# Attention's values, queries and keys kept split in DRAM, its mask tables made by GpSimd in the first FFN, and the softmax division on VectorE

## The chip, the core and the metric

The kernel runs on one core of one Trainium2 chip. The core has a matrix engine (TensorE, PE in the profile), a vector engine (VectorE, DVE), an activation engine (ScalarE, ACT), a general engine (GpSimd, POOL), a queue engine (SyncE, SP) that here only issues transfers, and 16 DMA engines. Each engine takes its instructions strictly in order, and waits on semaphores for the others. The metric is the device time of one execution in microseconds, as the median of several runs.

## What is computed

One layer of an encoder on 1024 tokens of width 1024, all in float32. The part that the change touches is the token mixer:

```python
h = h + 0.5 * swiglu(rms_norm(h, ffn1_norm), ffn1_w_gate, ffn1_w_up, ffn1_w_down)
u = rms_norm(h, mix_norm)
q, k, v, s_in, gates = split(u @ w_in)            # 512, 512, 512, 512, 2048 columns
y_attn = neighbourhood_attention(q, k, v, na_rpb) @ w_attn_out
y_ssm = s5_branch(s_in, ...) @ w_ssm_out
g_attn, g_ssm = split(sigmoid(gates))
h = h + (g_attn * y_attn + g_ssm * y_ssm) @ w_out
h = h + 0.5 * swiglu(rms_norm(h, ffn2_norm), ffn2_w_gate, ffn2_w_up, ffn2_w_down)
h = h + (p @ ple_w_proj) * sigmoid(rms_norm(h, ple_norm) @ ple_w_gate)
return rms_norm(h, final_norm)
```

The tokens are a grid of 16 rows by 64 columns. In neighbourhood_attention each of 8 heads of 64 dimensions lets a token see a window of 8 rows by 16 columns, clamped at the grid's edge, with a learned bias by relative position:

```python
bias = rpb[:, dr_idx[:, None, None], dc_idx[None]]
sc = einsum('bchd,brcwhd->bhcrw', qr, kn) * scale + bias
pr = softmax(sc)                                   # over the 8 x 16 window
out = einsum('bhcrw,brcwhd->bchd', pr, vn)
```

## The kernel before

A float32 product is made of three matmuls on operands that are split in two: hi, a rounded copy (CAST on ScalarE), and lo, the rest (a subtraction on VectorE), and then hi by hi, lo by hi and hi by lo (`mm3`, lines 184 to 186; `split`, lines 153 and 154). So each weight or activation tile costs one ScalarE and one VectorE operation before TensorE can use it. The first FFN runs from 0 to about 645 us, the mixer's projections, attention and SSM to about 1100 us, the merge and the output projection behind them, then the second FFN and the rest.

*The FFN* (`Ffn.run`) works through a list of items. In its second half an item is "B", one of 7 products by one of 11 blocks of the down projection: 12 matmuls on one tile araw (read back from a_d, split into ah and al) and one tile of weights (wblk, combined by additions in lines 422 and 424, then split into wh and wl). Each loop turn first issues the loads of items up to 7 ahead, then the preparation of items up to 4 ahead, then the item's matmuls, with a call of `tick()` after each three.

*Side work.* `tick()` counts down for one Python generator, which yields the number of ticks until its next piece. In the first FFN that generator is `gen_all`, which makes the SSM's tables with GpSimd (lines 918 to 933), pair by pair. In the mixer it is the attention and SSM generator: for each pair of heads and each unit of 16 it records a score (two matmuls, s), a softmax, a transposition (pt) and, two to five units later, the product with the values (O). The order in PE, DVE and ACT follows what the recording and the scheduler made of it.

*The mixer.* The values are made token tile by token tile (8 tiles of 24 matmuls, lines 1392 to 1394), copied by ScalarE into vs and stored in v_d. The query and key projections of a head pair follow (`qk_proj`), between tiles of the gates (gt). Queries and keys stay in SBUF: qs holds a head's high half in one half of the partitions and its low half in the other, and kh and kl hold the key's halves twice. For each head and column block `load_v` reads vf from v_d and splits it into vhl. `make_tabs` makes for each of the 16 units of 8 heads and 2 row blocks the bias and mask tables: row = bt + rowm (128 x 384), and three times tb = row + colm (288, 384 and 288 elements used), on VectorE in lines 1186 and 1193. A unit is then: s, the sum with tb and the maximum (L1211), the exponential (L1214), the reciprocal (L1215), the division as a ScalarE copy with a scale (L1216). During the first part of attention GpSimd runs the SSM's recurrence, 128 steps of three operations (`scan_steps`, lines 1092 to 1094), and in the last quarter `ssm_out` copies its states to xs and makes yo.

Rings matter here: `st` has 3 buffers of 128 x 1024 (staged weights, wst), `w` has 12 of 128 x 1024 (qs, kh, kl, weights, xs), and `tmp` has 4.

Of the kernel before, what the change touches and what calls it, by code (L numbers as in the profile page):

```python
# [16 lines left out]
P = 128  # L17
SEQ = 1024
# [11 lines left out]
KC0 = (0, 8, 24, 40)  # L30
KNC = (24, 32, 32, 24)
KVAR = (0, 1, 1, 2)
KF0 = (8, 0, 0, 0)
NEG = -1.0e30
PRI = 300

# [2 lines left out]
def encoder_block(ctx, tc, I, out):  # L39
# [35 lines left out]
    def tw(name, shape=(P, 1024), dt=F32R):  # L75
        return at("w", shape, dt, name)
# [13 lines left out]
    def dtile(name, shape):  # L90
        return dr.tile(list(shape), F32, name=name)
# [96 lines left out]
    def hsl(t):  # L188
        return slice(t * HT, (t + 1) * HT)
# [554 lines left out]
        return vecs.pop()  # L744

    def gconst(name, shape):
        return pools["g"].tile(list(shape), F32, name="g_" + name)

    def exp_parts(x, nm):

# [19 lines left out]
    def gen_params():  # L770
# [209 lines left out]
    def gen_all():  # L980
        while "g" not in pools:
            yield 1
        yield from gen_params()
        load_bc(0)
        yield 10
        for pr in range(NPAIR):
            fin = gen_pair(pr)
            yield 25 if pr < NPAIR - 2 else 40
            fin()
            yield 4  # L990

    def store_h(m, t):
        nc.scalar.dma_start(h_d[:, (2 * m + t) * HT:(2 * m + t + 1) * HT], h[m][t])
# [1 line left out]
    u, done, u_first, u_second = halves(h, 1, store_h)  # L995

    def t0_done():
        start(u_first())

    ffn = Ffn(s7, I["wg1"], I["wu1"], I["wd1"], a1_d, load_x, done, t0_done, (4, 7))  # L1000
# [122 lines left out]
        return go  # L1123


    rowm = const("rowm", [P, 2, 12])
    colm = const("colm", [P, 3, 32])
    nc.sync.dma_start(rowm, I["rowm"])
    nc.sync.dma_start(colm, I["colm"])
    vdr = v_d.rearrange("(r c) d -> r c d", c=GRID)  # L1130
    qkv = {}
    vld, tabs = {}, {}

    def qk_proj(hp, wq, wk):
        qs, kh, kl = [], [], []
        for t in range(2):
            o = proj(wq, t, "q")
            for i in range(2):
                if t == 0:
                    qs.append(tw("qs"))  # L1140
                src = o[i * 64:(i + 1) * 64].rearrange("p (r b c) -> p r b c", r=8, b=4)
                hs, ls = slice(i * 64, (i + 1) * 64), slice((1 - i) * 64, (2 - i) * 64)

                def view(sl):
                    return qs[i][sl, hsl(t)].rearrange("p (b r c) -> p r b c", b=4, r=8)
                A.copy(view(hs), src)
                V.tensor_tensor(view(ls), src, view(hs).bitcast(F32), ALU.subtract)
        for t in range(2):
            o = proj(wk, t, "k")
            for i in range(2):  # L1150
                if t == 0:
                    kh.append(tw("kh"))
                    kl.append(tw("kl"))
                hs, ls = slice(i * 64, (i + 1) * 64), slice((1 - i) * 64, (2 - i) * 64)
                A.activation(kh[i][hs, hsl(t)], o[hs], AF.Copy, scale=0.125)
                A.activation(kh[i][ls, hsl(t)], o[hs], AF.Copy, scale=0.125)
                for s_ in (hs, ls):
                    V.scalar_tensor_tensor(kl[i][s_, hsl(t)], o[hs], 0.125, kh[i][hs, hsl(t)].bitcast(F32),
                                           ALU.mult, ALU.subtract)
        for i in range(2):  # L1160
            qkv[2 * hp + i] = (qs[i], kh[i], kl[i])

    def load_v(hd, cb):
        n = 4 * KNC[cb]
        vf = tmp("vf", [P, 4, 64])
        for g in range(4):
            nc.sync.dma_start(vf[0:n, g],
                              vdr[4 * g:4 * g + 4, KC0[cb]:KC0[cb] + KNC[cb], hd * 64:(hd + 1) * 64])
        hl = thid("vhl", [P, 4, 2, 64])
        A.copy(hl[0:n, :, 0], vf[0:n])  # L1170
        V.tensor_tensor(hl[0:n, :, 1], vf[0:n], hl[0:n, :, 0].bitcast(F32), ALU.subtract)
        vld[hd, cb] = hl

    bts = {}

    def load_bias(b):

        if b < 2 * NH:
            e0 = 4 - 4 * (b % 2)
            bts[b] = ap_.tile([P, 12, 32], F32, tag="bt", bufs=1, name="bt")  # L1180
            nc.sync.dma_start(bts[b].rearrange("p r c -> p (r c)"), I["rpbw"][b // 2, :, e0 * 32:(e0 + 12) * 32])

    def make_tabs(hd, rb):
        b = 2 * hd + rb
        row = tmp("row", [P, 12, 32])
        V.tensor_tensor(row, bts.pop(b),
                        rowm[:, rb].unsqueeze(2).broadcast_to([P, 12, 32]), ALU.add)
        load_bias(b + 1)
        res = []
        for v in range(3):  # L1190
            n, f0 = (24, 32, 24)[v], (8, 0, 0)[v]
            tb = ap_.tile([P, 12, 32], F32, tag="tb", bufs=3, name="tb")
            V.tensor_tensor(tb[:, :, 0:n], row[:, :, f0:f0 + n],
                            colm[:, v, f0:f0 + n].unsqueeze(1).broadcast_to([P, 12, n]), ALU.add)
            res.append(tb)
        tabs[hd, rb] = res

    def attn_scores(hd, rb, cb):
        q, kh, kl = qkv[hd]
        n = KNC[cb]  # L1200
        nk = 12 * n
        qv = q[:, rb * HT + cb * P:rb * HT + (cb + 1) * P]

        def kv(kt):
            return kt.rearrange("p (r c) -> p r c", c=GRID)[:, 4 * rb:4 * rb + 12, KC0[cb]:KC0[cb] + n]
        s3 = bank("s")[:, 0:nk].rearrange("p (r c) -> p r c", c=n)
        T.matmul(s3, lhsT=qv, rhs=kv(kh), start=True, stop=False)
        T.matmul(s3, lhsT=qv, rhs=kv(kl), start=False, stop=True)
        sm = thid("sm", [P, 384], F32)[:, 0:nk]
        st = ap_.tile([P, 4], F32, tag="stat", bufs=4, name="stat")  # L1210
        V.tensor_tensor_reduce(out=sm.rearrange("p (r c) -> p r c", c=n), in0=s3,  # L1211
                               in1=tabs[hd, rb][KVAR[cb]][:, :, 0:n], scale=-1.0, scalar=3.0e38,
                               op0=ALU.add, op1=ALU.min, accum_out=st[:, 0:1])
        A.activation(sm, sm, AF.Exp, bias=st[:, 0:1], scale=-1.0, accum_out=st[:, 1:2])  # L1214
        V.reciprocal(st[:, 2:3], st[:, 1:2])  # L1215
        A.activation(sm, sm, AF.Copy, scale=st[:, 2:3])  # L1216
        return sm

    def attn_turn(cb, sm):
# [10 lines left out]
    def attn_values(hd, rb, cb, O, ph, pl):  # L1230
        kp = 4 * KNC[cb]
        hl = vld[hd, cb]
        for g in range(3):

            T.matmul(O[:, ksl(cb)], lhsT=hl[0:kp, rb + g].rearrange("p h d -> p (h d)"), rhs=ph[0:kp, ksl(g)], start=(g == 0), stop=False,
                     skip_group_check=True)
            T.matmul(O[0:64, ksl(cb)], lhsT=hl[0:kp, rb + g, 0], rhs=pl[0:kp, ksl(g)], start=False, stop=(g == 2),
                     skip_group_check=True)
        if cb == 3:
            ot, ol = tmp("ot"), tmp("ol")  # L1240
            A.copy(ol[0:64], O[64:128])
            V.tensor_tensor(ot[0:64].rearrange("p (r b c) -> p b r c", r=8, b=4),
                            O[0:64].rearrange("p (b r c) -> p b r c", b=4, r=8),
                            ol[0:64].rearrange("p (b r c) -> p b r c", b=4, r=8), ALU.add)
            nc.scalar.dma_start(o_d[hd * 64:(hd + 1) * 64, hsl(rb)], ot[0:64])
# [40 lines left out]
    def mixer_side():  # L1286
# [6 lines left out]
        for pr in range(NPAIR):  # L1293
# [7 lines left out]
                ld[pr + 1] = inject_load(pr + 1)  # L1301
            inject(pr, *ld.pop(pr))
            yield 3
        while 0 not in qkv:
# [12 lines left out]
        SO = 48  # L1317
        for j in range(n + 6):
            if j < n:
                hd, rb, cb = units[j]  # L1320
                while hd not in qkv:
                    yield 1
                if cb == 0 and j > 0:
                    make_tabs(hd, rb)
# [61 lines left out]
    for tt in range(NK):  # L1386
        o = bank("v")
        t, c0 = tt // 4, (tt % 4) * P
        for k in range(NK):
# [3 lines left out]
            T.matmul(o, lhsT=xh, rhs=wl, start=False, stop=False)  # L1393
            T.matmul(o, lhsT=xl, rhs=wh, start=False, stop=(k == NK - 1))
            tick()
        vs = tmp("vs")
        A.copy(vs, o)
        nc.scalar.dma_start(v_d[tt * P:(tt + 1) * P, :], vs)

    def load_br(t, b):  # L1400

# [30 lines left out]
            res += [(hi[:, ksl(k)], lo[:, ksl(k)]) for k in range(4)]  # L1432
        return res

    gm = 2
    for hp in range(4):
        wq, wk = loadw(win[hp]), loadw(win[4 + hp])
        w = loadw(win[16 + gm])
        qk_proj(hp, wq, wk)
        n = 2 if hp < 3 else 6  # L1440
        for i in range(n):
            wn = loadw(win[17 + gm]) if i < n - 1 else None
            for t in range(2):
                gate_tile(w, gm, t)
            gm += 1
            w = wn
    W = [loadw(win[16 + m]) for m in (14, 15)]
    for i in range(2):
        gate_tile(W[i], 14 + i, 0)
# [360 lines left out]
```

## Time and profile before

| | |
|---|---|
| median of 3 runs | 2099.88 us (2098.8 to 2100.49) |
| profiled execution, span | 2094.5 us |
| runs' median above that span | 5.4 us |
| TensorE busy | 2074.5 us |
| VectorE, ScalarE, GpSimd busy | 1416.1, 999.6, 399.4 us |
| DMA | 285.19 MB, mean 136 GB/s |

The span is what the profiler saw from the first to the last instruction of one execution; a run's time has a few microseconds around it. In the views a row names the line of the kernel, the engine, the operation, the tile written and the tiles read, the shape, and how often; "idle before" is the engine's gap just ahead, with what ended it. A matmul is listed with 0.39 us though the next one starts 0.23 us later, since they are pipelined.

### The profile page before, as it was taken

The numbers are of one execution on the slowest core, as the hardware profiler recorded it, in microseconds if no ns is written. First come the engines' busy times: TensorE is split into PE (matmuls) and PEld (weight loads), VectorE is DVE, ScalarE is ACT, GpSimd is POOL, SyncE is SP. The second block draws the span as 40 slices with busy tenths as digits, with TensorE's granted clock in tenths as the row PEclk, the third lists the DMA queues.
The fourth block names the chain that finished last, engine by engine and source line by source line (L and its number), as shares of the span: only waits on it lengthen the run. The fifth ranks groups of instructions, "written<-read, shape, count | busy, mean of one in ns | idle before, by whom it ended". The sixth has DMA issues, their size and how long they took to land.

```text
span 2094.5 us, 28063 instructions
## 1 busy us (share of the span) xinstructions
PE 2074.5 (99%) x9662; PEld 1705.4 (81%) x9662; DVE 1416.1 (68%) x2420; ACT 999.6 (48%) x1832; POOL 399.4 (19%) x636
## 2 busy tenths in 40 slices
PE   8999999999999999999999999999999999999998
PEld 3788888888888888888898888788888888888886
DVE  7897776667967334677753668995665665786855
ACT  6434333334445333667774635643333334445543
POOL 0037556441000006888200001000000000000000
PEclk9999999999999999999999999999999999999999
DMA  3435444475533551233477745243324238433302
GB/s 134 143 118 154 125 135 120 144 270 169 188 114 111 159 189 64 70 97 98 123 208 260 247 145 117 77 150 121 100 86 135 82 121 297 155 106 94 118 21 81
DMA packets 197744, 285.19 MB, mean 136 GB/s; under 512 B 41569, under 2 KB 81121, under 8 KB 197601
## 3 DMA queue, kind: packets, MB, share of 16 engines
q1 hardware_dynamic: 180304, 258.20, 38.8%
q10 hardware_dynamic: 14992, 21.00, 3.0%
q0 software_dynamic: 2304, 4.20, 1.2%
q8 instruction: 76, 1.25, 0.2%
q14 instruction: 68, 0.55, 0.1%
HBM read 201.01 MB, written 82.31 MB: 135 GB/s over the span
## 4 chain that ended last, share of the span: by engine, by line
PE 94%; DVE 2%; ACT 1%; DMA 1%; SPq 0%; issue 0%; DVEq 0%; ACTq 0%
PE dx L184 4%; PE dx L185 4%; PE dx L186 4%; PE gx L184 3%; PE ux L184 3%; PE ux L186 3%; PE gx L186 3%; PE gx L185 3%; PE ux L185 3%; PE gt L184 3%; PE gt L185 3%; PE gt L186 3%; PE dy L186 2%; PE dy L184 2%; PE dy L185 2%; PE gy L184 2%
## 5 line engine op out<-in xcount | busy, mean ns | idle before, releaser
L153 ACT CAST wh<-hbuf 128x512 fp32r<-128x512 f32 x280 | 173.0, 622 | 392.3 <-PE gx L185 80.9
L154 DVE TENSOR_TENSOR wl<-hbuf,wh 128x512 fp32r<-128x512 f32 x280 | 209.2, 750 | 122.7 <-ACT wh L153 120.5
L153 ACT CAST wh<-wblk 128x512 fp32r<-128x512 f32 x190 | 118.0, 622 | 192.6 <-PE dx L185 83.2
L154 DVE TENSOR_TENSOR wl<-wblk,wh 128x512 fp32r<-128x512 f32 x190 | 130.6, 690 | 49.3 <-ACT wh L153 41.8
L184 PE MATMUL dx<-ah,wh 128*128 128x512 f32 x416 | 163.3, 393 | 0.3 <-DVE hbuf L688 0.3
L186 PE MATMUL dx<-ah,wl 128*128 128x512 f32 x416 | 161.9, 389 | 0.0
L185 PE MATMUL dx<-al,wh 128*128 128x512 f32 x416 | 161.8, 389 | 0.0
L1092 POOL TENSOR_TENSOR sc<-X,rho 128x128 f32<-128x128 f32 x128 | 77.9, 609 | 327.2 <-ACT X L1075 317.3
L154 DVE TENSOR_TENSOR al<-araw,ah 128x512 fp32r<-128x512 f32 x154 | 106.3, 694 | 50.1 <-PE dx L185 21.1
L184 PE MATMUL gx<-xh,wh 128*128 128x512 f32 x320 | 124.9, 390 | 1.2 <-DVE c L575 1.2
L184 PE MATMUL ux<-xh,wh 128*128 128x512 f32 x320 | 125.0, 390 | 0.0
L186 PE MATMUL ux<-xh,wl 128*128 128x512 f32 x320 | 124.5, 389 | 0.0
L185 PE MATMUL gx<-xl,wh 128*128 128x512 f32 x320 | 124.5, 389 | 0.0
L186 PE MATMUL gx<-xh,wl 128*128 128x512 f32 x320 | 124.5, 389 | 0.0
L185 PE MATMUL ux<-xl,wh 128*128 128x512 f32 x320 | 124.5, 389 | 0.0
L153 ACT CAST ah<-araw 128x512 fp32r<-128x512 f32 x154 | 94.9, 619 | 43.2 <-PE dx L185 12.6
L184 PE MATMUL gt<-xh,wh 128*128 128x512 f32 x256 | 102.7, 401 | 0.0
L186 PE MATMUL gt<-xh,wl 128*128 128x512 f32 x256 | 99.8, 390 | 0.0
L185 PE MATMUL gt<-xl,wh 128*128 128x512 f32 x256 | 99.8, 390 | 0.0
L422 DVE TENSOR_TENSOR hbuf<-hbuf 128x512 f32<-128x512 f32 x120 | 91.4, 762 | 2.1
L184 PEld LDWEIGHTS dx<-ah,wh 128*128 128x128 f32 x416 | 78.1, 188 | 17.8 <-issue 0.7
L185 PEld LDWEIGHTS dx<-al,wh 128*128 128x128 f32 x416 | 78.1, 188 | 16.9 <-issue 0.7
(381 smaller groups left out, 5590.2 us busy)
## 6 DMA issues: line engine op xcount, KB each, us to landing
araw<-a_d SPq DMA_DIRECT2D x154, 256.0 KB
a_d<-c SPq DMA_DIRECT2D x148, 256.0 KB
wblk<-in_wd SPq DMA_DIRECT2D x88, 256.0 KB
hbuf<-in_wg SPq DMA_DIRECT2D x40, 512.0 KB
hbuf<-in_wu SPq DMA_DIRECT2D x40, 512.0 KB
wst<-in_win SPq DMA_DIRECT2D x26, 512.0 KB
hbuf<-in_xT SPq DMA_DIRECT2D x32, 256.0 KB
h_d<-hbuf ACTq DMA_DIRECT2D x32, 256.0 KB
```

Of the source, the lines that this page charges most:

```text
L153: A.copy(hi, src)
L154: return eng.tensor_tensor(lo, src, hi.bitcast(F32), ALU.subtract)
L184: T.matmul(o, lhsT=wh, rhs=xh, start=first, stop=False, skip_group_check=more)
L185: T.matmul(o, lhsT=wh, rhs=xl, start=False, stop=False, skip_group_check=more)
L186: T.matmul(o, lhsT=wl, rhs=xh, start=False, stop=last, skip_group_check=more)
L422: V.tensor_tensor(b11, (b12, b22, None, None, b21)[i - 2], b11, ALU.subtract)
L1092: G.tensor_tensor(sc, both, rho4, ALU.mult)
```

## The change

Four things change. Values, queries and keys are split once, straight behind their projections, and stored as halves: v_d doubles in width, q_d and k_d are new, and attention loads the halves (vhl, qs, kh, kl) from there without any copy. The value tile vs is now 128 x 1024 and comes from the `st` ring. The mask tables are made by GpSimd in the first FFN, behind the SSM's tables, stored in t_d, and loaded by attention (`load_tabs`). The division of the softmax moves from ScalarE to VectorE. And the order of query and key projections and gate tiles becomes a list, `todo`, in which the second head pair is projected earlier.

```diff
@@ -112,7 +115,10 @@
-    v_d = dtile("v_d", [SEQ, 512])
+    v_d = dtile("v_d", [SEQ, 1024])
+    q_d = dtile("q_d", [4, 2, P, SEQ])
+    k_d = dtile("k_d", [4, 2, P, SEQ])
+    t_d = dtile("t_d", [2 * NH, P, TABS])
@@ -877,6 +883,25 @@
+    def load_bias(b):
+
+        e0 = 4 - 4 * (b % 2)
+        bt = pools["g"].tile([P, 12, 32], F32, tag="tg", bufs=1, name="bt")
+        nc.sync.dma_start(bt.rearrange("p r c -> p (r c)"), I["rpbw"][b // 2, :, e0 * 32:(e0 + 12) * 32])
+        return bt
+
+    def gen_tabs(b, bt):
+
+        rb = b % 2
+        row = pools["g"].tile([P, 12, 32], F32, tag="em", bufs=1, name="row")
+        G.tensor_tensor(row, bt, gen["rowm"][:, rb].unsqueeze(2).broadcast_to([P, 12, 32]), ALU.add)
+        for v in range(3):
+            n, f0 = TN[v], TF0[v]
+            tb = pools["g"].tile([P, 12 * n], F32, tag=("gm", "pg", "pe")[v], bufs=1, name="to")
+            G.tensor_tensor(tb.rearrange("p (r c) -> p r c", c=n), row[:, :, f0:f0 + n],
+                            gen["colm"][:, v, f0:f0 + n].unsqueeze(1).broadcast_to([P, 12, n]), ALU.add)
+            nc.sync.dma_start(t_d[b, :, TOFF[v]:TOFF[v] + 12 * n], tb)
@@ -988,6 +1013,16 @@
...
+        for b in range(2 * NH):
+            bt = load_bias(b)
+            yield 4
+            gen_tabs(b, bt)
+            yield 4
@@ -995,6 +1030,7 @@
     def t0_done():
+        drain()
         start(u_first())
@@ -1123,77 +1159,58 @@
...
     def qk_proj(hp, wq, wk):
-        qs, kh, kl = [], [], []
         for t in range(2):
             o = proj(wq, t, "q")
...
+            hi, lo = tmp("qh", dt=F32R), tmp("ql", dt=F32R)
...
+            A.copy(view(hi), src)
+            V.tensor_tensor(view(lo), src, view(hi).bitcast(F32), ALU.subtract)
+            for i, x in enumerate((hi, lo)):
+                nc.scalar.dma_start(q_d[hp, i, :, hsl(t)], x.bitcast(F32))
         for t in range(2):
             o = proj(wk, t, "k")
...
+            hi, lo = tmp("kh", dt=F32R), tmp("kl", dt=F32R)
+            A.activation(hi, o, AF.Copy, scale=0.125)
+            V.scalar_tensor_tensor(lo, o, 0.125, hi.bitcast(F32), ALU.mult, ALU.subtract)
+            for i, x in enumerate((hi, lo)):
+                nc.scalar.dma_start(k_d[hp, i, :, hsl(t)], x.bitcast(F32))
+        ready.update((2 * hp, 2 * hp + 1))
+
+    def load_qk(hd):
+        hp, ds = hd // 2, slice((hd % 2) * 64, (hd % 2 + 1) * 64)
+        qs, kh, kl = tw("qs"), tw("kh"), tw("kl")
         for i in range(2):
-            qkv[2 * hp + i] = (qs[i], kh[i], kl[i])
+            hs = slice(i * 64, (i + 1) * 64)
+            nc.sync.dma_start(qs[hs].bitcast(F32), q_d[hp, i, ds])
+            nc.sync.dma_start(kh[hs].bitcast(F32), k_d[hp, 0, ds])
+            nc.sync.dma_start(kl[hs].bitcast(F32), k_d[hp, 1, ds])
+        qkv[hd] = (qs, kh, kl)
 
     def load_v(hd, cb):
         n = 4 * KNC[cb]
-        vf = tmp("vf", [P, 4, 64])
+        hl = thid("vhl", [P, 4, 2 * 64])
         for g in range(4):
-            nc.sync.dma_start(vf[0:n, g],
-                              vdr[4 * g:4 * g + 4, KC0[cb]:KC0[cb] + KNC[cb], hd * 64:(hd + 1) * 64])
-        hl = thid("vhl", [P, 4, 2, 64])
-        A.copy(hl[0:n, :, 0], vf[0:n])
-        V.tensor_tensor(hl[0:n, :, 1], vf[0:n], hl[0:n, :, 0].bitcast(F32), ALU.subtract)
+            nc.sync.dma_start(hl[0:n, g].bitcast(F32),
+                              vdr[4 * g:4 * g + 4, KC0[cb]:KC0[cb] + KNC[cb], hd * 128:(hd + 1) * 128])
         vld[hd, cb] = hl
...
@@ -1207,13 +1224,15 @@
...
         V.reciprocal(st[:, 2:3], st[:, 1:2])
-        A.activation(sm, sm, AF.Copy, scale=st[:, 2:3])
+        V.tensor_scalar(sm, sm, st[:, 2:3], None, ALU.mult)
@@ -1301,27 +1320,32 @@
...
-        load_bias(0)
-        make_tabs(0, 0)
-        scan_steps(4)
-        yield 6
+        load_tabs(0)
+        load_qk(0)
+        for _ in range(5):
+            scan_steps(1)
+            yield 2
...
+                if hd not in qkv:
+                    load_qk(hd)
+                if rb == 0 and cb == 2 and hd + 1 in ready:
+                    load_qk(hd + 1)
+                if cb == 0:
+                    load_tabs(2 * hd + rb + 1)
@@ -1393,9 +1417,12 @@
-        vs = tmp("vs")
-        A.copy(vs, o)
-        nc.scalar.dma_start(v_d[tt * P:(tt + 1) * P, :], vs)
+        vs = at("st", [P, 1024], F32R, "vs")
+        vv = vs.rearrange("p (h a d) -> p h a d", h=NH, a=2)
+        ov = o.rearrange("p (h d) -> p h d", h=NH)
+        A.copy(vv[:, :, 0], ov)
+        V.tensor_tensor(vv[:, :, 1], ov, vv[:, :, 0].bitcast(F32), ALU.subtract)
+        nc.scalar.dma_start(v_d[tt * P:(tt + 1) * P, :], vs.bitcast(F32))
@@ -1432,18 +1459,24 @@
...
+    todo = [("qk", 0), ("g", 2), ("qk", 1), ("g", 3), ("g", 4), ("qk", 2), ("g", 5), ("g", 6), ("qk", 3)]
+    todo += [("g", m) for m in range(7, 14)]
...
```

SyncE's queue in the down projection of the first FFN, before: of the loads for that stage (araw from a_d, wblk from the weights) the last 42 araw loads stand with nothing between them.

```order
L602 DMA araw<-a_d 128x512 x3
L601 DMA wblk<-in_wd 128x512 x7
...
L602 DMA araw<-a_d 128x512
L601 DMA wblk<-in_wd 128x512 x2
L602 DMA araw<-a_d 128x512 x42
```

The same queue of the change, in the part where the sets of tables begin (bt is the bias that a set reads, to a finished table, e_d an SSM table):

```order
L608 DMA araw<-a_d 128x512 x11
L890 DMA bt<-in_rpbw 128x384
L608 DMA araw<-a_d 128x512
L903 DMA t_d<-to 128x288
L988 DMA e_d<-ka 16x8x128 x2
L903 DMA t_d<-to 128x384
L903 DMA t_d<-to 128x288
L608 DMA araw<-a_d 128x512
L903 DMA t_d<-to 128x288
L608 DMA araw<-a_d 128x512
L890 DMA bt<-in_rpbw 128x384
```

Between the loads of araw now stand, for each of 16 sets, one load and three stores, and each store waits for GpSimd.

GpSimd's queue behind its last SSM work, before it goes on with the recurrence; in the kernel before nothing stands there. One set of the change (row, then the three tables):

```order
L897 TENSOR_TENSOR row<-bt,g_rowm 128x384
L901 TENSOR_TENSOR to<-row,g_colm 128x288
L901 TENSOR_TENSOR to<-row,g_colm 128x384
L901 TENSOR_TENSOR to<-row,g_colm 128x288
```

Sixteen such sets are added there.

ScalarE's order among the value tiles (vs), before: the two casts wh<-wst in the middle are those of the first query and key weights, and they stand behind the second of eight value tiles.

```order
L1397 COPY vs<-v 128x512
L1398 DMA v_d<-vs 128x512
L1397 COPY vs<-v 128x512
L1398 DMA v_d<-vs 128x512
L153 CAST wh<-wst 128x1024 x2
L1397 COPY vs<-v 128x512
L1398 DMA v_d<-vs 128x512
```

And of the change, at the last two of the eight value tiles, where these two casts are the first of five in a row:

```order
L1423 CAST vs<-v 128x8x64
L1425 DMA v_d<-vs 128x1024
L1423 CAST vs<-v 128x8x64
L1425 DMA v_d<-vs 128x1024
L159 CAST wh<-wst 128x1024 x5
L1176 CAST qh<-q 128x8x4x16
L1179 DMA q_d<-qh 128x512
L1179 DMA q_d<-ql 128x512
```

The casts of the first query and key weights have moved from behind the second value tile to behind the eighth and its store.

More of the change, by code (lines that the diff above doesn't have):

```diff
@@ L32 @@
 KVAR = (0, 1, 1, 2)
-KF0 = (8, 0, 0, 0)
+TN = (24, 32, 24)
+TF0 = (8, 0, 0)
+TOFF = (0, 288, 672)
+TABS = 960
 NEG = -1.0e30
@@ L746, in gconst @@
     def gconst(name, shape):
-        return pools["g"].tile(list(shape), F32, name="g_" + name)
+        return pools["g"].tile(list(shape), F32, tag=name, bufs=1, name="g_" + name)
     def exp_parts(x, nm):
@@ L1132, in encoder_block, with view @@
     vld, tabs = {}, {}
+    ready = set()
     def qk_proj(hp, wq, wk):
-        qs, kh, kl = [], [], []
         for t in range(2):
             o = proj(wq, t, "q")
[L1138 to L1147, printed above, removed]
+            hi, lo = tmp("qh", dt=F32R), tmp("ql", dt=F32R)
+            def view(x):
+                return x.rearrange("p (b r c) -> p r b c", b=4, r=8)
+            src = o.rearrange("p (r b c) -> p r b c", r=8, b=4)
+            A.copy(view(hi), src)
+            V.tensor_tensor(view(lo), src, view(hi).bitcast(F32), ALU.subtract)
+            for i, x in enumerate((hi, lo)):
+                nc.scalar.dma_start(q_d[hp, i, :, hsl(t)], x.bitcast(F32))
@@ L1148, in qk_proj @@
         for t in range(2):
             o = proj(wk, t, "k")
[L1150 to L1159, printed above, removed]
@@ L1172, in load_v, with load_tabs @@
         vld[hd, cb] = hl
-    bts = {}
-    def load_bias(b):
+    def load_tabs(b):
         if b < 2 * NH:
[L1179 to L1196, printed above, removed]
+            for v in range(3):
+                n = 12 * TN[v]
+                tabs[b, v] = ap_.tile([P, 384], F32, tag="tb", bufs=4, name="tb")[:, 0:n]
+                nc.sync.dma_start(tabs[b, v], t_d[b, :, TOFF[v]:TOFF[v] + n])
@@ L1233, in attn_values @@
         for g in range(3):
-            T.matmul(O[:, ksl(cb)], lhsT=hl[0:kp, rb + g].rearrange("p h d -> p (h d)"), rhs=ph[0:kp, ksl(g)], start=(g == 0), stop=False,
+            T.matmul(O[:, ksl(cb)], lhsT=hl[0:kp, rb + g], rhs=ph[0:kp, ksl(g)], start=(g == 0), stop=False,
                      skip_group_check=True)
-            T.matmul(O[0:64, ksl(cb)], lhsT=hl[0:kp, rb + g, 0], rhs=pl[0:kp, ksl(g)], start=False, stop=(g == 2),
+            T.matmul(O[0:64, ksl(cb)], lhsT=hl[0:kp, rb + g, 0:64], rhs=pl[0:kp, ksl(g)], start=False, stop=(g == 2),
                      skip_group_check=True)
@@ L1303, in mixer_side @@
             yield 3
-        while 0 not in qkv:
+        while 0 not in ready:
             scan_steps(1)
@@ L1320, in mixer_side @@
                 hd, rb, cb = units[j]
-                while hd not in qkv:
+                while hd not in ready:
                     yield 1
-                if cb == 0 and j > 0:
-                    make_tabs(hd, rb)
+                if hd not in qkv:
[4 more added lines that the diff above has]
+                    load_tabs(2 * hd + rb + 1)
                 sms[j] = attn_scores(hd, rb, cb)
@@ L1433, in load_was, with task_w @@
         return res
[L1435 to L1446, printed above, removed]
+    todo = [("qk", 0), ("g", 2), ("qk", 1), ("g", 3), ("g", 4), ("qk", 2), ("g", 5), ("g", 6), ("qk", 3)]
+    todo += [("g", m) for m in range(7, 14)]
+    def task_w(n):
+        if n < len(todo):
+            kind, m = todo[n]
+            return [loadw(win[x]) for x in ((m, 4 + m) if kind == "qk" else (16 + m,))]
+    wn = task_w(0)
+    for n, (kind, m) in enumerate(todo):
+        w, wn = wn, None
+        if kind == "qk":
+            wn = task_w(n + 1)
+            qk_proj(m, *w)
+            continue
+        wn = task_w(n + 1)
+        for t in range(2):
+            gate_tile(w[0], m, t)
     W = [loadw(win[16 + m]) for m in (14, 15)]
```

13 lines of the change are left out of this document (8 added, 5 removed).

## The prediction

> **What bounds the kernel now.** I read the page first: the span, the busy shares, the forty slices, then the chain that ended last.
>
> ```profile
> span 2094.5 us, 28063 instructions
> PE 2074.5 (99%) x9662; PEld 1705.4 (81%) x9662; DVE 1416.1 (68%) x2420; ACT 999.6 (48%) x1832; POOL 399.4 (19%) x636
> PE   8999999999999999999999999999999999999998
> PEclk9999999999999999999999999999999999999999
> PE 94%; DVE 2%; ACT 1%; DMA 1%; SPq 0%; issue 0%; DVEq 0%; ACTq 0%
> ```
>
> TensorE is busy for 2074.5 of 2094.5 us, with the clock granted in full in every slice. Every other engine has idle time on average. So a change can win only what TensorE waits, and the waits of TensorE come next: engine, line and tile that waited, what it waited for, us in total, times, longest.
>
> ```profile
> PE g L651 <- ACT xg L336: 5.0, 1, 5.0
> PE gx L184 <- DVE c L575: 1.2, 1, 1.2
> PE yo L1117 <- DVE ot L1242: 0.7, 1, 0.7
> PE yo L1117 <- DMA emi<-u_d: 0.4, 1, 0.4
> ```
>
> The two large ones stand in the first 100 us, at a place that the change leaves alone. In the mixer only the two rows of yo are there, **1.1 us together**: all that a lighter ScalarE or VectorE in attention could give back. The matrix multiplications stay the same in number and size (the order of the built programs has 9058 rows on TensorE before and after). Therefore the case is one-sided: the gain is at most about 1.1 us, and the question is which new waits appear.
>
> **Part 1: the tables, now made by GpSimd during the down projection of the first FFN.** There are 16 sets, one every 8 ticks; each has a row operation of 384 elements and three tables of 288, 384 and 288. A tick is three matmuls, and these start 0.227 us apart (22 of them between 830.19 and 835.18, the rows of part 3), so the sets spread over 16 x 8 x 0.68 = 87 us behind the last table of the SSM, which ends near 505 us. First the view of that stretch in pieces (busy PE, PEld, DVE, ACT, POOL with their instructions, clock, DMA share, GB/s):
>
> ```profile
> 505.00:540.00 35.00, 35.00 (x156) 29.00 (x155) 22.24 (x38) 16.75 (x30) 0.00 (x0) 1.00 0.55 170
> 540.00:580.00 40.00, 40.00 (x178) 33.10 (x178) 40.00 (x67) 17.18 (x31) 0.00 (x0) 1.00 0.48 164
> 580.00:595.00 15.00, 15.00 (x68) 12.43 (x67) 11.39 (x20) 6.55 (x12) 0.00 (x0) 1.00 0.33 98
> ```
>
> GpSimd is empty here, which makes the place look free. But VectorE is busy for 22.24 + 40.00 + 11.39 = 73.6 of 90 us, and from 540 to 580 without a gap. What a GpSimd instruction does to VectorE is read earlier, where both work (the timeline of each engine near 165 us), beside the same VectorE operations with GpSimd idle (groups of 505 to 595):
>
> ```profile
> 165.00 1.88 POOL L920 TENSOR_TENSOR em<-em,tg 128x576 f32<-128x576 f32 x1
> 165.69 1.21 DVE L959 SCALAR_TENSOR_TENSOR ka<-g_dm,g_dk,ka 32x16 f32<-32x16 f32 x1
> ...
> L959 DVE SCALAR_TENSOR_TENSOR ka<-g_dm,g_dk,ka 32x16 f32<-32x16 f32 x1 | 0.2, 217 | 0.0
> L154 DVE TENSOR_TENSOR al<-araw,ah 128x512 fp32r<-128x512 f32 x34 | 23.1, 681 | 0.8 <-issue 0.8
> L422 DVE TENSOR_TENSOR wblk<-wblk 128x512 f32<-128x512 f32 x28 | 18.9, 679 | 0.0
> ```
>
> A VectorE operation of 217 ns took 1.21 us: it started at 165.69 and ended at 166.90, when GpSimd's ended (165.00 + 1.88 = 166.88). The reverse stands in the mixer: a GpSimd operation of 0.32 us took 1.18 us beside a VectorE subtraction (rows 808.38, 806.07 and 805.64 below). So the two engines take turns, one instruction each, when both have two operands in SBUF. Nearly everything VectorE does in this stretch is of that kind (L154, L422).
>
> The Trainium skill, "GPSIMD Engine Reference", section "1. Specifications", says that GpSimd shares its SBUF interfaces with VectorE and contends with VectorE's two-SBUF-input and 2-port instructions. The traces above agree for the first kind; without the rule, two engines side by side would make this part cost 0, and with it the sum below holds.
>
> Now the price of a set, from the nearest GpSimd forms (minimum, median and maximum in ns):
>
> ```profile
> L918 POOL TENSOR_TENSOR gm<-g_pg,bb x16: 1054/1078/1598, 144.4 to 470.3; 128x512 f32<-128x512 f32 x16
> L920 POOL TENSOR_TENSOR gm<-gm,tv x16: 1286/1300/1741, 152.9 to 479.4; 128x512 f32<-128x512 f32 x16
> ```
>
> The new additions take one broadcast operand, like L918: 1054/512 = 2.06 ns per element, so a set of 1344 elements is 2.77 us and 16 sets are 44 us. By L920, which reads two full operands, it is 2.51 ns, 3.38 us and 54 us. GpSimd waits for the end of the VectorE instruction in progress and starts some 0.13 us ahead of that end (in the fence below, 805.64 + 1.43 = 807.07 against 806.07 + 1.18 - 0.32 = 806.93), so of each of the 64 instructions about 0.13 us is hidden: VectorE is held for 44 - 8 = **36 us**, or 46. It has 90 - 73.6 = 16.4 us free. The rest is 19.6 us, or 29. Against it stands a lead: the code prepares operands four items ahead, an item being 12 matmuls or 2.72 us, so at most 10.9 us. What VectorE lacks beyond that, TensorE waits: **8.7 us, or 18.7** by the dearer form; if the gapless stretch from 540 to 580 has already eaten the lead, 19.6 to 29. If a table instruction costs under 0.56 us on average (64 x (0.56 - 0.13) = 27.3 = 16.4 + 10.9), it is 0. I take **10 us**, near L918's form, whose operands look most like the new ones. SyncE's queue is in order, and each table's store waits there for GpSimd with later loads of araw behind it; these are issued seven items or 19 us ahead, and a set takes 5.2 us even when each of its four instructions lets one VectorE instruction of 0.6 us pass, so I add nothing.
>
> **Part 2: the values.** Here are the last value tile and the first query projection, with the second of the two casts and subtractions of query and key weights that stood far ahead of it (776.58), and a later weight subtraction beside GpSimd (805.64):
>
> ```profile
> 775.50 1.05 ACT L153 CAST wh<-wst 128x1024 fp32r<-128x1024 f32 x1 [0.46 <-DMA wst<-in_win]
> ...
> 776.58 1.23 DVE L154 TENSOR_TENSOR wl<-wst,wh 128x1024 fp32r<-128x1024 f32 x1 [0.29 <-ACT wh L153]
> ...
> 805.64 1.43 DVE L154 TENSOR_TENSOR wl<-wst,wh 128x1024 fp32r<-128x1024 f32 x1 [7.78 <-ACT wh L153]
> 806.07 1.18 POOL L1093 TENSOR_TENSOR sc<-sc 128x64 f32<-128x64 f32 x1
> 808.38 0.32 POOL L1093 TENSOR_TENSOR sc<-sc 128x64 f32<-128x64 f32 x1
> 808.43 0.39 PE L1394 MATMUL v<-wh,xl 128*128 128x512 f32 x1
> 808.66 0.39 PE L184 MATMUL q<-xh,wh 128*128 128x512 f32 x1
> 808.86 0.59 ACT L1397 COPY vs<-v 128x512 f32<-128x512 f32 x1 [3.25 <-PE v L1394]
> 809.48 0.33 ACTq L1398 DMA_DIRECT2D v_d<-vs  x1
> ...
> L688 DVE SCALAR_TENSOR_TENSOR hbuf<-dx,hbuf 128x512 f32<-128x512 f32 x8 | 5.0, 682 | 0.0
> ```
>
> Before, these weights were cast and subtracted by 777.8, thirty us ahead, and TensorE went from v to q in 0.23 us. Now vs draws from the three buffers that the weights are staged in, and in ScalarE's new order all casts of the query weights stand behind the eighth value copy and its store. The store in turn waits for VectorE's subtraction. The chain from the last v matmul's start: copy begins 0.43 later (808.86), lasts 0.59, the subtraction with one operand in PSUM 0.68 (L688's kind, the last row of the fence), the store's issue 0.33, the cast 1.05: q can start after 3.08 instead of 0.23 us, 2.85 late. Its third matmul needs the low half, 1.23 us after the cast (the row of 776.58), less the 0.45 us of two matmuls: 0.78 more. **3.6 us**, with nothing beside it, since TensorE is in order. It falls to 0 only if the casts were not behind the store; up to 5 if the staged weights, too, land late.
>
> **Part 3: queries and keys through DRAM.** No row has q_d or k_d, so the nearest round trip is that of v_d:
>
> ```profile
> 813.06 1.19 SPq L1167 DMA_DIRECT2D vf<-v_d  x2
> 815.56 0.41 ACT L1170 CAST vhl<-vf 96x256 fp32r<-96x256 f32 x1 [6.12 <-DMA vf<-v_d]
> 830.19 0.39 PE L186 MATMUL k<-xh,wl 128*128 128x512 f32 x1
> 835.18 0.29 PE L1207 MATMUL s<-kh,qs 128*128 128x288 f32 x1
> ```
>
> The store issued at 809.48 released the load at 813.06 (3.58 us), and its data were used at 815.56 (2.50 us). In the new chain kh's copy starts 0.43 us after the last k matmul and lasts 0.59, kl takes 0.68, and its store is issued at 1.70; the load of kl is released at 5.28; three more loads stand behind it at 0.33 to 0.6 each, and the last lands 2.50 later, at 8.8 to 9.6. The new program has 33 gate matmuls before the first score, which would start at 34 x 0.227 = 7.7. So TensorE waits 1.1 to 1.9 us; I take **1.5**, with 0 and 4 as ends (six loads of 256 KB are ten times the bytes of vf's). Later heads are loaded half a head ahead or more and cost nothing.
>
> **Part 4: the softmax division on VectorE, and the copies that go.**
>
> ```profile
> L1216 ACT ACTIVATE sm<-sm,stat x64: 525/577/619, 839.1 to 1088.3; 128x288 f32<-128x288 f32 x32, 128x384 f32<-128x384 f32 x32
> L1111 ACT COPY xs<-X x32: 388/403/409, 1015.3 to 1080.3; 64x256 f32<-64x256 f32 x32
> 800.00:1015.00 215.00, 215.00 (x1204) 185.24 (x1203) 144.94 (x329) 136.26 (x294) 180.48 (x381) 1.00 0.28 82
> ```
>
> ScalarE loses 64 x 0.58 us, VectorE gains as many operations and loses 64 table operations and 32 splits. From 800 to 1015 TensorE is never idle, so all that relief is worth nothing there. Behind 1015 it may remove the 1.1 us of waits. Against that, a whole head's qs, kh and kl now sit in the ring of 12 that xs shares; where xs must wait for its slot, up to four copies of 0.40 and a cast of 1.05 pile up ahead of the attention work in ScalarE's queue, 2.65 us at a place, twice at most. I take **0**, between -1.1 and +5.3. The transfers (some 42 MB more) are on a queue with a share of 0.28 to 0.55 and cost nothing by themselves.
>
> **Sum.** 10 + 3.6 + 1.5 + 0 = 15.1. The span of 2094.5 becomes 2109.6. The median of the runs, 2099.88, lies 5.4 above the profiled span; with that the time is **2115.0 us**.
>
> **Rivals.** *Tables hidden* (0.24): VectorE's gaps and lead take all of part 1, because the additions are cheaper than 0.56 us each. For it speaks the stretch in which GpSimd makes the SSM's tables:
>
> ```profile
> 60.00:505.00 445.00, 443.79 (x2023) 362.69 (x2022) 337.74 (x552) 180.04 (x351) 203.16 (x232) 1.00 0.49 155
> ```
>
> GpSimd worked 203 us there, and TensorE lost 1.2 us, none of it to a held-up subtraction. Against it: VectorE, whose 337.74 us already hold what GpSimd cost it, had 107 of 445 us left there, and in the new place 16.4 of 90 before GpSimd begins. 2099.9 + 5.1 = 2105.0. *Not slower* (0.12): the tables are hidden as above, and the keys return within the 7.7 us, and the two yo waits go; the point is a round trip of under 5 us from kl's store instead of 6.1 plus the queue. Only part 2 is left: 2099.9 + 3.6 - 1.1 = 2102.4, within 0.2%, and under it if the cast's wait is shorter. *Tables dear* (0.16): L920's price, or a lead already spent: 2099.9 + 18.7 to 29 + 5.1 = 2124 to 2134, say 2128. *The change misses its aim*, since nothing moved was on the path: it is in all of these.
>
> **Chances.** The forecast has 0.48. The measurement can tell some 0.2%, 4.2 us, from no change: slower means over 2104.1, faster under 2095.7. Tables hidden falls on both sides of 2104.1, mostly above. Slower 0.84, same 0.13, faster 0.03 (an effect not seen here, since only 1.1 us of waits can go). The range of 2102 to 2130 leaves out the dearer half of the dear case and a part of the not-slower one.
>
> **What would show it.** Part 1: in the new profile TensorE waits between 550 and 600 us for wl, al or ah, VectorE's L160 mean there is well over 681 ns, and GpSimd's rows come singly between VectorE's. If the waits are absent and VectorE only fills its gaps, part 1 is wrong. Part 2: a wait of 3 to 4 us of q at L190 to L192 near 810 us for wh or wl. Part 3: a wait of s at L1224 of 1 to 2 us for the loads of k_d. Part 4: waits of O or yo behind 1015 us. A clock under full, or an idle TensorE in the second FFN, would be outside all of this.

## The result, and the profile after

| | before | after |
|---|---|---|
| median of 4 runs | 2099.34 us | 2136.1 us (2134.81 to 2138.43) |
| ratio | 1 | 1.0175, 95% interval 1.0161 to 1.019 |
| profiled span | 2094.5 us | 2133.7 us |

The change is 36.8 us slower by the medians and 39.2 by the spans; the two differ since the profiled execution before lies 5.4 us under the median of its runs and that of the change 2.4. Slower was forecast, 2115 was the number, and 2130 the end of the range: the sign held and the size was too small by more than half. The page after the change, span, engines, TensorE's line of the forty slices and the chain:

```profile
span 2133.7 us, 28295 instructions
PE 2088.2 (98%) x9662; PEld 1710.2 (80%) x9662; DVE 1407.7 (66%) x2364; ACT 936.9 (44%) x1704; POOL 478.6 (22%) x700
PE   8999999999889999999989999999999999999998
PE 83%; DVE 6%; DMA 5%; POOL 2%; ACT 2%; issue 1%; SPq 1%; DVEq 0%; ACTq 0%; POOLq 0%
```

TensorE's matmuls are 9662 as before, but they are busy for 13.7 us more (2088.2 against 2074.5), and idle time grew from 20.0 to 45.5 us. The idle time is in the list of TensorE's waits (what waited, what for, us in total, times, longest):

```profile
PE q L190 <- ACT wh L159: 4.9, 1, 4.9
...
PE dx L191 <- DVE al L160: 3.6, 4, 2.0
PE dx L192 <- DVE wl L160: 2.9, 4, 1.3
PE O L1254 <- ACT pth L1245: 2.4, 1, 2.4
PE dy L191 <- DVE al L160: 2.3, 1, 2.3
PE yo L1153 <- DMA emi<-u_d: 2.3, 2, 1.2
PE s L1225 <- DMA kl<-k_d: 1.9, 1, 1.9
...
PE O L1256 <- DVE ptl L1246: 1.7, 1, 1.7
PE dy L190 <- ACT ah L159: 1.4, 1, 1.4
```

All four parts of the forecast are there: dx and dy in the down projection, q behind v, the first s, and O and yo in the last quarter. What was not in the forecast is the extra busy time. The clock explains most of it: these are stretches of the same trace just before, in and just behind one of them (busy PE, PEld, DVE, ACT, POOL, then the granted clock, DMA share, GB/s):

```profile
545.00:550.60 5.60, 1.83 (x7) 1.00 (x6) 2.87 (x5) 3.22 (x6) 2.89 (x4) 1.00 0.88 284
550.70:554.00 3.30, 3.30 (x9) 2.55 (x8) 3.30 (x7) 1.76 (x3) 0.00 (x0) 0.50 1.00 363
554.20:558.00 3.80, 3.80 (x19) 3.09 (x18) 3.80 (x7) 2.41 (x5) 3.03 (x1) 1.00 1.06 395
```

Behind a stretch in which TensorE mostly waited, the granted clock is 0.50 for 3.4 us, and a matmul starts every 0.43 instead of 0.227 us. The trace has five such stretches, at 550.7, 605.3, 834.0, 868.1 and 1090.0 us, each behind a wait of about 2 us or more; the kernel before has none between its first 20 us and its end. One costs half of 3.4 us, 1.7, and the five cost 8.5 of the 13.7 us. At least a part of the rest is the matmul ahead of each wait, which is listed as busy for 0.39 us where the next one could have started after 0.23.

To place the loss I add up, from the starts of all matmuls, each distance to the next one less the median distance of the same pair of kinds in the kernel before (us by stage; a clock at half counts in it). Before the change a stage already has some, since not all pairs alike are equally far apart:

```
                     up-proj.  down-proj.  s_in to v  q, k  attention  last quarter
before                  6.7        0.4        2.4      0.0     5.4         3.4
after                   7.8       18.6        3.0      7.2     8.9        12.2
difference              1.1       18.2        0.6      7.2     3.5         8.8
of it at half clock      -         3.4         -       1.7     1.7         1.7
```

The differences sum to 39.4 us, the growth of the span within 0.2. The 1.1 us of the up-projection is one wait (ms at L351), which differs from run to run: 0.8 us before, 1.8 here, 0.3 and 2.2 in two of the runs below. The experiments take these stages one at a time, and each is read by its stage as well as by its time, because runs of one kernel differ by 4 us and more here. Each run of a kernel stands beside the kernel before on the same chip, at medians of 2097.9 to 2098.9 us.

### The profile page after: what moved, and what is told of

Same layout as the page of the kernel before. It is cut to its first block, busy times and chain, and to the rows that moved or that the text cites. A ratio compares the mean times of both kernels' runs of the same rounds, so it can differ in the third digit from the quotient of the medians.

```text
span 2133.7 us, 28295 instructions
## 1 busy us (share of the span) xinstructions
PE 2088.2 (98%) x9662; PEld 1710.2 (80%) x9662; DVE 1407.7 (66%) x2364; ACT 936.9 (44%) x1704; POOL 478.6 (22%) x700
## 4 chain that ended last, share of the span: by engine, by line
PE 83%; DVE 6%; DMA 5%; POOL 2%; ACT 2%; issue 1%; SPq 1%; DVEq 0%; ACTq 0%; POOLq 0%
PE dx L190 3%; PE dx L192 3%; PE dx L191 3%; PE ux L190 3%; PE ux L191 3%; PE ux L192 3%; PE gx L190 3%; PE gx L191 3%; PE gx L192 3%; PE gt L190 3%; PE gt L192 3%; PE gt L191 3%; PE dy L192 2%; PE dy L190 2%; PE dy L191 2%; PE gy L190 2%
## 5 line engine op out<-in xcount | busy, mean ns | idle before, releaser
L160 DVE TENSOR_TENSOR wl<-wblk,wh 128x512 fp32r<-128x512 f32 x190 | 138.2, 730 | 32.2 <-ACT wh L159 26.2
L160 DVE TENSOR_TENSOR al<-araw,ah 128x512 fp32r<-128x512 f32 x154 | 114.9, 750 | 53.2 <-PE dx L191 21.1
L1128 POOL TENSOR_TENSOR sc<-X,rho 128x128 f32<-128x128 f32 x128 | 71.8, 561 | 215.9 <-ACT X L1111 205.9
L192 PEld LDWEIGHTS dx<-ah,wl 128*128 128x128 f32 x416 | 78.4, 188 | 21.3 <-DVE wl L160 5.1
```

Of the source, the lines that this page charges most:

```text
L160: return eng.tensor_tensor(lo, src, hi.bitcast(F32), ALU.subtract)
L192: T.matmul(o, lhsT=wl, rhs=xh, start=False, stop=last, skip_group_check=more)
L1128: G.tensor_tensor(sc, both, rho4, ALU.mult)
```

## The experiments

**The first feed-forward stage.** Three theories: the two engines hold each other up; SyncE's queue, where loads of araw stand behind stores that wait for GpSimd; both. First the queue was taken out:

```diff
-            nc.sync.dma_start(t_d[b, :, TOFF[v]:TOFF[v] + 12 * n], tb)
+            nc.gpsimd.dma_start(t_d[b, :, TOFF[v]:TOFF[v] + 12 * n], tb)
```

and the same for the load of bt.

> The bias loads and the table stores of the first FFN go on GpSimd's own queue instead of SyncE's; the table operations stay. Queue theory (loads of araw stand behind stores that wait for GpSimd, and that alone makes TensorE wait): the 18.6 us lost in the down projection nearly vanish, 2136 to about 2118 us, and ScalarE no longer waits 28.7 us for araw. Turn-taking theory (GpSimd holds VectorE up): the loss stays between 10 and 18 us, 2128 to 2136. Both coupled: some 8 to 12 us stay, about 2127, with waits for al and wl but none for ah.

The median was 2135.9 us, but the four runs lie from 2128.6 to 2143.7, so the time tells nothing. The profiled one is the fastest, and its down projection lost 10.5 us, with waits for al and wl and none for ah. That looked like "both". Then the second operand was taken out:

```diff
-        G.tensor_tensor(row, bt, gen["rowm"][:, rb].unsqueeze(2).broadcast_to([P, 12, 32]), ALU.add)
+        G.tensor_copy(row, bt)
```

and likewise for the three tables; this kernel leaves out the masks.

> The 64 additions on GpSimd become copies with one operand, so the masks are left out; loads, stores and their queue stay as they are. Turn-taking of two-operand instructions: GpSimd and VectorE no longer hold each other up, VectorE's subtractions are back at 681 ns, and the 18.6 us vanish: about 2118. Queue theory by itself: GpSimd still takes 0.5 to 0.8 us an operation and the loads still stand behind its stores, 2130 to 2136. If a copy holds VectorE too, nothing changes: 2136.

2117.3 us (ratio 1.0087, 1.0072 to 1.0102), and the down projection lost 0.4 us as before the change. Transfers, stores that wait for GpSimd, loads of araw behind these and 64 GpSimd instructions were all still there, so these need not cost anything; with the additions the stage lost over SyncE's queue and over GpSimd's. But the edit changed two more things: a copy is shorter than an addition (at the least 0.43 us against 0.79 for the same table), and the scheduler ordered SyncE's queue in another way, with the first load of wblk at 530.73 us, among the stores, instead of at 544.93, behind 23 of them. So this run does not tell the second operand from the length or from the order.

The trace of the changed kernel shows two kinds of loss. The first is the wait at 545 to 550 us with the half clock behind it, 6 of the 18 us. There VectorE was not held up but idle; its weights were late (rows of SyncE, VectorE and ScalarE):

```profile
538.30 3.04 SPq L903 DMA_DIRECT2D t_d<-to  x3
543.15 1.74 SPq L903 DMA_DIRECT2D t_d<-to  x2
544.93 1.58 SPq L607 DMA_DIRECT2D wblk<-in_wd  x3
```

```profile
547.73 0.86 DVE L428 TENSOR_TENSOR wblk<-wblk 128x512 f32<-128x512 f32 x1 [4.06 <-DMA wblk<-in_wd]
549.12 0.68 DVE L160 TENSOR_TENSOR al<-araw,ah 128x512 fp32r<-128x512 f32 x1
```

```profile
546.34 0.62 ACT L159 CAST ah<-araw 128x512 fp32r<-128x512 f32 x1 [2.22 <-DMA t_d<-to]
```

In the kernel before, the first load of wblk went out at 524.92 us, and in the run over GpSimd's own queue at 525.82; neither has this wait. So it came by SyncE's queue. The other 12 us lie from 576 to 620 us, and from 580 on VectorE is busy there without a gap. How GpSimd's additions meet VectorE's instructions there is shown by the two timelines, with starts and durations in us (a row with x2 or x3 holds that many instructions):

```profile
593.31 3.77 POOL L901 TENSOR_TENSOR to<-row,g_colm 128x288 f32<-128x288 f32 x3
597.16 1.16 POOL L897 TENSOR_TENSOR row<-bt,g_rowm 128x384 f32<-128x384 f32 x1
598.40 3.76 POOL L901 TENSOR_TENSOR to<-row,g_colm 128x288 f32<-128x288 f32 x3
```

```profile
593.71 1.29 DVE L428 TENSOR_TENSOR wblk<-wblk 128x512 f32<-128x512 f32 x1
594.92 2.71 DVE L160 TENSOR_TENSOR wl<-wblk,wh 128x512 fp32r<-128x512 f32 x2
597.55 1.32 DVE L160 TENSOR_TENSOR al<-araw,ah 128x512 fp32r<-128x512 f32 x1
598.79 2.71 DVE L428 TENSOR_TENSOR wblk<-wblk 128x512 f32<-128x512 f32 x2
601.42 1.28 DVE L160 TENSOR_TENSOR wl<-wblk,wh 128x512 fp32r<-128x512 f32 x1
```

Six VectorE instructions take from 593.71 to 601.42, 1.28 us each. In the kernel before, with GpSimd idle, they start 0.60 us apart:

```profile
541.01 0.68 DVE L154 TENSOR_TENSOR al<-araw,ah 128x512 fp32r<-128x512 f32 x1
541.61 0.68 DVE L154 TENSOR_TENSOR wl<-wblk,wh 128x512 fp32r<-128x512 f32 x1
```

GpSimd's come at the same 1.27 us: one by one, as forecast. But 38 us earlier the same program did something else:

```profile
546.29 1.75 POOL L901 TENSOR_TENSOR to<-row,g_colm 128x288 f32<-128x288 f32 x2
554.97 14.15 POOL L901 TENSOR_TENSOR to<-row,g_colm 128x288 f32<-128x288 f32 x1 [6.93 <-DMA t_d<-to]
569.21 0.83 POOL L897 TENSOR_TENSOR row<-bt,g_rowm 128x384 f32<-128x384 f32 x1
```

```profile
557.31 0.33 SPq L608 DMA_DIRECT2D araw<-a_d  x1
569.16 0.33 SPq L903 DMA_DIRECT2D t_d<-to  x1
569.53 1.40 SPq L607 DMA_DIRECT2D wblk<-in_wd  x3
571.03 0.38 SPq L608 DMA_DIRECT2D araw<-a_d  x1
```

One GpSimd addition, 0.8 us by itself, took 14.15 us, while VectorE ran its own back to back. The store of its table and all loads behind it on SyncE stood still from 557.6 to 569.2. From 575 to 612 ScalarE waited 24.3 us in all for araw. Whether this stop cost TensorE anything is not shown. In the run with copies one copy was held as long, SyncE's queue stood still behind it from 557.3 to 569.8, and TensorE lost nothing:

```profile
555.67 14.13 POOL L897 COPY row<-bt 128x384 f32<-128x384 f32 x1 [6.05 <-DMA bt<-in_rpbw]
```

The tables' other place was tried by giving them back to VectorE in attention:

```diff
-            bt = load_bias(b)
-            yield 4
-            gen_tabs(b, bt)
-            yield 4
...
+        V.tensor_tensor(row, bts.pop(b), rowm[:, b % 2].unsqueeze(2).broadcast_to([P, 12, 32]), ALU.add)
```

> The tables are made by VectorE within attention as before the change; nothing is added to the first FFN; all other edits stay. If all of the down projection's loss comes from the tables: 2136 - 18.6 = 2117.5 us, and TensorE is without waits from 505 to 700. Rival: VectorE's table work returns to attention and costs there: 2120 or more, with longer waits behind 1040 us.

2117.4 us (1.0088, 1.0073 to 1.0103), with 0.4 us lost in the down projection and the last quarter at 11.4 instead of 12.2. VectorE has the time for 64 table operations in attention; making them elsewhere saved nothing.

**The values.** Two tiles of another ring in place of one of the st ring:

```diff
-        vs = at("st", [P, 1024], F32R, "vs")
+        for q in range(2):
+            vs = thid("vs")
...
+            nc.scalar.dma_start(v_d[tt * P:(tt + 1) * P, hsl(q)], vs.bitcast(F32))
```

> The value halves go to two 128 x 512 tiles of another ring (two copies, two subtractions and two stores for each value tile), so that the staged weights have the st ring to themselves. If the ring is the cause: q no longer waits 5.1 + 0.8 us, and the 3.4 us at half clock behind it go too, 2136 - 7.2 = 2129. Rival: the query weights land late since SyncE's queue holds their loads behind those of vhl: a wait of 2 to 3 us stays, 2132.

The time moved by 4 us, 2132.0 (2129.0 to 2137.3); the stage by all of its 7.2, to 0.0, and q no longer stands in the list of waits. The ring is the cause of the wait. The rival's late weights were a consequence of the same ring, as the changed kernel's ScalarE shows:

```profile
828.75 0.58 ACT L1423 CAST vs<-v 128x512 fp32r<-128x512 f32 x1 [4.85 <-PE v L1418]
830.09 0.33 ACTq L1425 DMA_DIRECT2D v_d<-vs  x1
832.56 1.04 ACT L159 CAST wh<-wst 128x1024 fp32r<-128x1024 f32 x1 [3.22 <-DMA wst<-in_win]
```

Behind the last store ScalarE was not held by its order any more, but waited until 832.56 for the weights. SyncE issued their loads only from 826.89 on, behind twelve loads of vhl. With the other ring these loads went ahead of those of vhl, and ScalarE cast the first two query weights at 782.95 and 785.40. How much of the delay is a buffer that was not free, and how much the place in SyncE's queue that came with it, is not separated.

**Queries and keys.** Nine steps in place of five before the first score:

```diff
-        for _ in range(5):
+        for _ in range(9):
```

> Nine steps of two ticks instead of five between the first head's loads and the first score (5.4 us more of gate matmuls on TensorE in between). If the first score waits only for the round trip of the keys: its wait of 2.1 us and the 3.4 us at half clock behind it go, 3.6 us in all, 2136.1 to 2132.5. Rival: attention as a whole ends 5.4 us later against the gates, so that the last quarter is denser and gives it back: 2135 to 2138.

2131.2 us (1.0161, 1.0146 to 1.0176): attention's loss fell from 8.9 to 4.8, so that its growth of 3.5 is gone, and the half-clock stretch behind the first score is gone. The round trip of the keys is the cause there. The last quarter stayed at 10.9, now with a wait of 2.9 us for late gate weights.

**The last quarter.** xs in the large ring:

```diff
-        xs = tw("xs", [P, 2, 2, NCH], F32)
+        xs = thid("xs", [P, 2, 2, NCH], F32)
```

> The SSM's states xs go to the large ring of 128 x 512 tiles and no longer share the 12 buffers with the head's qs, kh and kl. If the shared ring makes the last quarter slow: ScalarE no longer waits 11.8 us for yo ahead of xs, the waits of O (2.4, 1.7, 0.6) go, and the stage loses 3 to 4 us as before the change instead of 12.2: 2136.1 to about 2128. Rival: the loads of emi are late in SyncE's queue behind the loads of the heads: O's waits go, yo's 2.3 us stay, 2131. If ScalarE's order alone is at fault: 2136.

The time is 2134.2 (2128.7 to 2136.6), too scattered to tell; the stage fell from 12.2 to 7.5, all waits of O are gone, and yo's 2.3 us for emi stayed: the rival's pattern. What the shared ring did is seen in the changed kernel's ScalarE, ahead of the wait of O for pth that ends at 1087.46:

```profile
1082.48 0.82 ACT L1147 COPY xs<-X 64x256 f32<-64x256 f32 x2 [3.42 <-PE yo L1155]
1083.33 0.37 ACT L1157 COPY ys<-yo 128x256 f32<-128x256 f32 x1
1083.73 0.37 ACTq L1158 DMA_DIRECT2D y_d<-ys  x1
1084.31 1.65 ACT L1147 COPY xs<-X 64x256 f32<-64x256 f32 x4 [0.61 <-PE gt L191]
1085.98 1.04 ACT L159 CAST wh<-wst 128x1024 fp32r<-128x1024 f32 x1
1086.93 0.47 ACT L1245 CAST pth<-pt 128x384 fp32r<-128x384 f32 x1
```

ScalarE sat for 3.42 us before a copy that needed a buffer held until yo was done; then four copies and a cast stood ahead of pth. The division was put back as well:

```diff
-        V.tensor_scalar(sm, sm, st[:, 2:3], None, ALU.mult)
+        A.activation(sm, sm, AF.Copy, scale=st[:, 2:3])
```

> The division of the softmax goes back to ScalarE; all else stays. The move was costed at nothing: 2136 within 1 us. If it relieved ScalarE where TensorE waits for pth: 1 to 3 us slower, 2138, in the last quarter. If VectorE's share of the last quarter is at fault: 1 to 2 us faster.

2135.7 us (2133.5 to 2136.6), with 12.6 us in the last quarter: in runs that lie 3 us apart, the division neither costs nor brings anything that shows.

**Together.** The four edits at once (tables on VectorE, values, later score, xs):

> Four edits together: tables by VectorE in attention as before, value halves in a ring of their own, the later first score, xs in the large ring. If these four places are all that the change lost, and do not hide one another: 2136.1 - 18.7 - 7.2 - 3.6 - 8.5 = 2098.1, level with the kernel before; no stretch at half clock is left. Rival: the places are coupled, and a wait taken away comes back further on: 2103 or more.

2103.0 us (1.0024, 1.0013 to 1.0036). Not level: the last quarter still lost 8.6, with yo waiting 1.5 us for emi, gates waiting 1.8 for weights, and one half-clock stretch. The sum of parts had hidden 5 us there. Two runs brought the tables back to GpSimd with the three mixer edits, once over SyncE and once over GpSimd's queue:

> The change with the three mixer edits (value halves in a ring of their own, later first score, xs in the large ring), tables by GpSimd in the first FFN with SyncE's queue as in the change. If part 1 is independent of the mixer, the time is that of the four edits together plus 18.2 to 19: 2121 to 2122 us. Rival: tables read back from DRAM also cost or save in attention: outside of 2119 to 2124.

> The same, with bias loads and table stores on GpSimd's own queue. If SyncE's queue adds to the turn-taking what the profile of the first such run showed (10.5 instead of 18.6 us lost in the down projection): 2113, 8 us under its neighbour. If the slow runs of that first try (2142) are the rule and the queue does not matter: 2121 or more.

2128.3 and 2132.8 us; the down projection lost 19.5 and 26.1. GpSimd's own queue is not faster, and the expectation of 2113 fell. In that run GpSimd was never held for more than 5.3 us (its table operations: minimum, median, maximum in ns), and VectorE paid in full:

```profile
L901 POOL TENSOR_TENSOR to<-row,g_colm x48: 795/1046/5287, 504.4 to 621.2; 128x288 f32<-128x288 f32 x32, 128x384 f32<-128x384 f32 x16
```

TensorE waited there for al once for 12.9 us. In the first run with that queue a GpSimd instruction had been held for 23.58 us, and the loss was 10.5. So with the additions the stage lost in both, whichever engine was held longest, and which one it is changes between programs that differ elsewhere only. The first of the two runs lost 14.8 us in the last quarter, against 8.6 with tables on VectorE. Its 48 loads of tables stand in SyncE's queue, too, but need not cost this, as the last run shows. The last two runs issued emi's loads one unit earlier:

```diff
+            if 0 <= j - SO + 1 < NPAIR:
+                pre[j - SO + 1] = load_emi(j - SO + 1)
```

> The four edits together, with the loads of emi issued one unit earlier. If the wait of yo for emi (1.5 us) is what is left of the last quarter beside the late gate weights (1.8 us and a half-clock stretch of 1.7): 2103.0 to 2101.5. Rival: the order of the queue only shifts the wait to vhl or the gate weights: 2103 to 2105. Nothing here can bring it under the kernel before by more than the 1.1 us of waits in attention.

> The change with all mixer edits (value halves in a ring of their own, later first score, xs in the large ring, emi loaded one unit earlier), tables by GpSimd in the first FFN as in the change. If the order of SyncE's loads (emi and weights behind vhl, tables and heads) is what remained of the last quarter, its 14.8 us fall to about 5, and only part 1 is left: 2100.9 + 18.2 = 2119 us. Rival: the tables' 48 loads delay the weights and emi wherever these stand: 2124 or more, with waits of gt for weights and of yo for emi.

With tables on VectorE: 2100.9 us of 11 runs (1.0007, 0.9998 to 1.0016), level with the kernel before, the last quarter at 4.7, and no half clock behind the first 20 us. With tables by GpSimd: 2120.5 (1.0108, 1.0091 to 1.0125), with 19.1 us in the down projection and 6.4 in the last quarter. The two differ in the tables only, by 19.6 us (20.0 when each is taken against the kernel before on its own chip).

## Why the prediction was wrong in size

**What bounds.** Right: nothing could be won, and all that was added is in new waits of TensorE and the half clock behind them.

**Part 1, 10 us; 18.2 lost.** Turn-taking was right, and its price was mis-sized at the step "near L918's form, whose operands look most like the new ones". That misread the code: L918 multiplies two broadcast operands, while each new addition has one. The shortest row operation takes 0.83 us, the shortest tables 0.79, 1.00 and 0.79, so a set takes 3.41 us at the least: the dearer L920's 3.38 and not L918's 2.77. The same sum with the dearer price was 18.7, and it stood in the text as the other end. That it meets 18.2 is luck, since the sum holds no half clock (3.4 us here) and no wait by way of the queue. "I add nothing" for SyncE's queue was the second step that failed: the first wait of this stage, 6 us with its half clock, stands where loads of wblk were behind stores of tables. For the rest of the loss that queue isn't needed, by the runs over GpSimd's queue. "The two engines take turns, one instruction each" is right for 593 to 612 us and wrong for 555 to 569, where GpSimd got none.

**Part 2, 3.6 us; 7.2 lost.** The order was read rightly, and the wait is 4.9 + 0.4 us on the list; the step that failed is the staging: the weights' own loads came late with the ring that vs now shares ("up to 5 if the staged weights, too, land late" was the end not taken). Half clock adds 1.7.

**Part 3, 1.5 us; 3.5 lost.** The wait is 1.9, within its 1.1 to 1.9. The rest is half clock.

**Part 4, 0; 8.8 lost.** The mechanism against the change was named with 2.65 us at a place, and then set to 0, although the range around it reached from -1.1 to +5.3. Of the 8.8, 4.7 went with the ring; with the other edits made, 3.9 (8.6 to 4.7) went with the order of emi's loads, which the prediction did not look at: loads of heads, tables and values stand ahead of them on SyncE.

**What was missing in every part.** "A clock under full ... would be outside all of this." Five stretches of 3.4 us at half clock cost some 8.5 us, a fifth of the loss. The Trainium skill, "TensorE: Matmul & The Clock Gate", section "Part 1: The HAM clock gate", has half rate as the state behind an idle window of about 3.4 us. The length of the half-clock stretches here agrees with that figure, 3.4 us, and in other runs they last 6.8 or 13.7; the condition is milder here, since waits of 2.1 us were enough. That price belonged behind every new wait of 2 us.

Of the rivals, *tables dear* (2124 to 2134) came nearest; what it lacked are the half clock behind the new waits and the last quarter, and its upper end comes near by luck, with 29 us for part 1.

## What to carry to other kernels

An engine that is idle is not free if its instructions take turns with those of a busy one: look at what the busy engine runs in that stretch, price the newcomer by the dearest similar instruction, and look for gaps in the busy engine, not in the idle one. When a tile moves to another ring or a result goes through DRAM, list what else draws from that ring and what stands behind its transfers in the queue; the losses in the mixer were all of this kind, and three of the four mixer edits that took them away only gave a tile another ring or a load an earlier place. And price a wait of TensorE of two microseconds as that wait plus a possible stretch at half clock behind it, 1.7 us here.

## What the runs showed of the chip that was not expected

VectorE running two-operand instructions back to back can shut GpSimd's out: one of 0.8 us lasted 14.15 us here, and 23.58 in the run over GpSimd's queue, while elsewhere in the same run the two alternate at 1.27 us a pair. What decides between the two wasn't tried. A copy with one operand was shut out as well, for 14.13 us. But copies hardly held VectorE up: in that run its subtractions were mostly at 0.68 us with a few at 0.91 to 0.99, and nothing was lost.

A wait of TensorE of about 2 us is at the edge for the clock (waits here are the delay of a matmul's start, some 0.2 us more than the list shows). In the changed kernel waits of 2.1 and 2.15 us were followed by half clock, and one of 1.58 was not; with the later score, waits of 2.16, 2.00 and 2.17 were not either. Where the longest wait behind the start was 1.54 us (the four edits with early emi) the clock stayed full. The length of one wait isn't all that counts: with the four edits alone, waits of 1.48 and 0.70 us within 3 us were followed by half clock. And the stretch is not always 3.4 us: it was 6.8 us behind several waits of the other runs, and 13.7 in and behind the wait of 12.9.
